# One encoder layer on one core: the up-projection by seven quarter products, activations parked in DRAM, the down-projection as three sweeps

## The chip, the core and the metric

The kernel runs on one core of a Trainium2 chip. The metric is the device time of one execution in microseconds (us). TensorE (PE) multiplies, VectorE (DVE), ScalarE (ACT) and GpSimd (POOL) work on its results, and SyncE (SP) issues the transfers between DRAM and the chip. All data are float32.

## The reference, cut to what matters

The program is one layer of a streaming encoder for 1024 prompt tokens and 32 sample tokens: an input projection, two kinds of attention, an output projection with a first norm, a gated feed-forward with a causal convolution of width 3, a second norm, and a gated embedding. The change concerns the feed-forward:

```python
def _conv_ffn(h, conv_state, lp):
    u = h @ lp['w_up']                       # (tokens, 1024) @ (1024, 5632)
    up = jnp.concatenate([conv_state, u], 1)
    z = lp['conv_b'] + sum(up[:, j:j + s] * lp['conv_w'][j] for j in range(CONV_W))
    g, v = z[..., :D_FF], z[..., D_FF:]      # D_FF = 2816
    out = (jax.nn.gelu(g, approximate=False) * v) @ lp['w_down']   # (tokens, 2816) @ (2816, 1024)
...
h = _ln(ALPHA * x + a, lp['ln1_g'], lp['ln1_b'])
f, new_conv = _conv_ffn(h, conv_state, lp)
h = _ln(ALPHA * h + f, lp['ln2_g'], lp['ln2_b'])
gate = jax.nn.sigmoid(h @ lp['w_ple_gate'] + lp['b_ple_gate'])
y = h + gate * (p_emb @ lp['w_ple_proj'])
```

## The kernel before

**Products.** TensorE reads its operands as float32r, a shorter form of float32. Each operand is therefore kept as two parts: `split` copies the high part on ScalarE (L85) and subtracts it from the source on VectorE or GpSimd (L82). `three` (L144 to L146) then sums three matmuls for each pair of 128x128 tiles: high by high, high by low, low by high.

**Layout.** Features lie on the partitions, tokens along the columns: 1024 prompt tokens, 2 spare columns and 32 sample tokens make T = 1058. On-chip memory is cut into pools: `G` (8 large tiles), `WP` (6 tiles of half that size, `pair`), `SL` (4, `slab`) and `ST` (2, `stg`). Every weight tile that `wload` brings in passes through one of the two `ST` buffers: a load (L112), a copy on ScalarE, a subtraction on VectorE or GpSimd; then the buffer is free again.

**Order.** A scheduler orders each engine's instructions when the program is built: what is written first goes first, as soon as its inputs and a buffer are there. Each engine then runs its list in that order and waits only for data and buffers. `held` and `load` keep an instruction, in that order, behind the one that `gate[0]` names.

**Up.** After the output projection, `h_rows` makes the normed rows of a block of 128 tokens (the two products with g and b of the norm run on GpSimd, L1038 and L1039, but for the last block), `h_cols` turns them on TensorE (L1068) and writes both parts into `hT`. The up-projection then takes 44 feature tiles, gate and value of a feature in turn. For each, `up_block` runs three blocks of 352 or 354 token columns, 24 matmuls each, with the weights as the stationary operand, and ScalarE copies the sum out (L1097). `conv` makes three VectorE operations of it (L1110, L1112). `glu` applies GELU and multiplies; `keep` splits the result into `acts`.

**Down.** Features are taken in groups of four. While the next group's up-projection runs, `down` multiplies the group before with its rows of w_down: for each block of tokens and each half of 512 columns, three matmuls per feature, then an addition into the row sums in `acc` on VectorE (L1153). So up- and down-projection alternate, and the weights of the one come in under the products of the other. Before the last stage, the weights of the gate are loaded (`wg`) while the last groups are multiplied.

**Last stage.** `y_norm` adds the last two features and norms the rows, `y_cols` turns and splits them, `y_rows` multiplies with the gate's weights and writes the output; six blocks of rows are normed ahead.

## Time and profile before

| what | us |
|---|---|
| median of 3 runs | 1627.09 (1626.44 to 1627.8) |
| span of the profiled execution | 1620.0 |
| TensorE busy in it | 1564.6 (97%) |
| VectorE, ScalarE, GpSimd busy | 843.5, 597.1, 352.3 |

The span runs from the first instruction to the last of one profiled execution; what that execution took outside its span is not recorded, so only the timed runs show it. "Busy" counts time in which an engine had at least one instruction under way. A matmul is pipelined: its duration in a row is longer than the distance to the next matmul, and it is that distance that adds up to time.

### The profile page before, as it was taken

To read this page: it belongs to the slowest core of one execution; us is meant where nothing else is said; L and a number is where in the kernel's file an instruction comes from. 1 tells how busy PE (TensorE), PEld (TensorE's weight loads), DVE (VectorE), ACT (ScalarE), POOL (GpSimd) and SP (SyncE) were. 2 spreads that over 40 slices of the span, in tenths; PEclk is the share of its full clock that TensorE was granted. 3 is DMA by queue.
4 is the path that set the end of the run, shared out by engine and by line. 5 is a ranking of instruction groups with operands and counts; after the bars stand their busy time and mean duration, and the time that the engine had idled before them with its cause. 6 is when DMAs were issued, how large, how long until landed. Compare 5 with 4: busy or idle time off the path is not lost.

```text
span 1620.0 us, 23579 instructions
## 1 busy us (share of the span) xinstructions
PE 1564.6 (97%) x9486; PEld 1429.8 (88%) x9486; DVE 843.5 (52%) x1505; ACT 597.1 (37%) x1339; POOL 352.3 (22%) x432
## 2 busy tenths in 40 slices
PE   8999998889989999999999999999999999999998
PEld 7999987778878899999979988997998899876887
DVE  4112328887777665755444443544444354688322
ACT  4222438887787750233303321330332133232111
POOL 0002225633464202810000000000000000038511
PEclk9999999999999999999999999999999999999999
DMA  7121252220111162011102111110211111140001
GB/s 238 44 59 41 79 166 46 63 54 8 45 43 37 31 226 55 27 53 53 40 13 79 40 39 53 53 40 13 79 40 40 52 53 40 40 156 17 35 34 40
DMA packets 95506, 95.58 MB, mean 59 GB/s; under 512 B 10733, under 2 KB 80997, under 8 KB 95141
## 3 DMA queue, kind: packets, MB, share of 16 engines
q1 hardware_dynamic: 95397, 94.07, 19.0%
q8 instruction: 75, 1.23, 0.3%
q14 instruction: 34, 0.28, 0.1%
HBM read 77.74 MB, written 9.96 MB: 54 GB/s over the span
## 4 chain that ended last, share of the span: by engine, by line
PE 81%; DVE 9%; ACT 4%; DMA 3%; POOL 1%; issue 1%; SPq 0%; ACTq 0%; DVEq 0%; POOLq 0%
PE pm L144 23%; PE pm L145 23%; PE pm L146 23%; PE pm L810 2%; DVE w L521 1%; DVE w L559 1%; DVE g L82 1%; PE pm L801 1%; PE pm L152 1%; PE pm L153 1%; ACT w L85 1%; PE pd L144 1%; DMA t<-in_w_o 1%; DVE w L82 1%; ACT g L85 1%
## 5 line engine op out<-in xcount | busy, mean ns | idle before, releaser
L144 PE MATMUL pm<-g,w 128*128 128x352 f32 (+2 forms) x1300 | 425.8, 328 | 2.4 <-DVE w L82 1.1
L145 PE MATMUL pm<-g,w 128*128 128x352 f32 (+2 forms) x1300 | 424.9, 327 | 0.1
L146 PE MATMUL pm<-g,w 128*128 128x352 f32 (+2 forms) x1300 | 422.3, 325 | 0.4 <-DVE w L82 0.4
L144 PE MATMUL pm<-w,g 128*128 128x256 f32 (+2 forms) x896 | 296.4, 331 | 5.7 <-DVE sm L176 3.0
L146 PE MATMUL pm<-w,g 128*128 128x256 f32 (+2 forms) x896 | 293.8, 328 | 0.4 <-DVE g L82 0.2
L145 PE MATMUL pm<-w,g 128*128 128x256 f32 (+2 forms) x896 | 293.1, 327 | 0.0
L144 PEld LDWEIGHTS pm<-g,w 128*128 128x128 f32 x1300 | 245.3, 189 | 5.5 <-DVE w L82 1.6
L145 PEld LDWEIGHTS pm<-g,w 128*128 128x128 f32 x1300 | 246.0, 189 | 1.6 <-DVE g L82 0.9
L146 PEld LDWEIGHTS pm<-g,w 128*128 128x128 f32 x1300 | 245.9, 189 | 1.6 <-DVE w L82 0.9
L144 PEld LDWEIGHTS pm<-w,g 128*128 128x128 f32 x896 | 169.9, 190 | 24.7 <-DVE sm L176 3.6
L85 ACT CAST w<-t 128x1024 fp32r<-128x1024 f32 (+2 forms) x97 | 100.9, 1041 | 228.0 <-PE pm L146 187.2
L146 PEld LDWEIGHTS pm<-w,g 128*128 128x128 f32 x896 | 168.6, 188 | 16.7 <-DVE g L82 1.0
L145 PEld LDWEIGHTS pm<-w,g 128*128 128x128 f32 x896 | 169.0, 189 | 15.5 <-issue 0.5
L1107 POOL COPY ucol<-s 128x2 f32<-128x2 f32 x44 | 31.5, 716 | 635.0 <-ACT s L1097 635.0
L1097 ACT COPY s<-pm 128x352 f32<-128x352 f32 x132 | 59.9, 454 | 279.9 <-PE pm L146 279.8
L82 DVE TENSOR_TENSOR w<-t,w 128x1024 fp32r<-128x1024 f32 (+2 forms) x91 | 111.2, 1222 | 97.1 <-ACT w L85 97.1
L1110 DVE TENSOR_SCALAR s<-s,cp 128x1058 f32<-128x1058 f32 x44 | 36.6, 832 | 232.5 <-ACT s L1097 232.5
L1112 DVE SCALAR_TENSOR_TENSOR s<-s,cp,s 128x1058 f32<-128x1058 f32 x88 | 115.9, 1318 | 1.6
L1153 DVE TENSOR_TENSOR g<-pm,g 128x512 f32<-128x512 f32 x96 | 64.6, 682 | 88.3 <-PE pm L146 88.2
L82 DVE TENSOR_TENSOR w<-pm,w 128x512 fp32r<-128x512 f32 (+3 forms) x124 | 61.3, 515 | 19.0 <-ACT w L85 18.4
L85 ACT CAST w<-pm 128x512 fp32r<-128x512 f32 (+3 forms) x124 | 53.2, 450 | 48.2 <-PE pm L801 18.6
L119 POOL TENSOR_SCALAR s<-s,sm 128x1024 f32<-128x1024 f32 (+8 forms) x56 | 45.3, 811 | 106.1 <-DVE sm L783 65.1
(291 smaller groups left out, 2386.6 us busy)
## 6 DMA issues: line engine op xcount, KB each, us to landing
t<-in_w_up SPq DMA_DIRECT2D x44, 512.0 KB, 3.7
t<-in_w_down SPq DMA_DIRECT2D x22, 512.0 KB, 3.2
g<-in_x_p SPq DMA_DIRECT2D x15, 512.0 KB, 9.7
t<-in_w_in SPq DMA_DIRECT2D x14, 512.0 KB, 3.8
t<-in_w_o SPq DMA_DIRECT2D x8, 512.0 KB
t<-in_w_gate SPq DMA_DIRECT2D x8, 512.0 KB, 3.3
out_y_p<-t SPq DMA_DIRECT2D x16, 256.0 KB, 2.0
g<-g SPq DMA_DIRECT2D x6, 512.0 KB, 4.3
```

The lines of the kernel that those rows point to most:

```text
L82: return eng.tensor_tensor(out, x, y, ALU.subtract)
L85: c = ACT.copy(hi, src)
L119: return eng.tensor_scalar(out, x, s, 0.0, ALU.mult, ALU.add)
L144: PE.matmul(ps, sh, mh, start=(i == 0), stop=False)
L145: PE.matmul(ps, sh, ml, start=False, stop=False)
L146: PE.matmul(ps, sl, mh, start=False, stop=(i == last))
L810: PE.matmul(po[:, c : c + 256], vt[:, k, h % 4], pts[k // 4][:, hl, k % 4], start=(k == 0 and hl == 0), stop=(k == kt - 1 and hl == 1))
L1097: ACT.copy(U[:, 2 + c0 : 2 + c0 + n], ps[:, :n])
L1107: POOL.tensor_copy(ucol[:, 0:2, m], U[:, 1024:1026])
L1110: DVE.tensor_scalar(z, U[:, 0:T], cp[:, 0, m : m + 1], cp[:, 3, m : m + 1], ALU.mult, ALU.add)
L1112: DVE.scalar_tensor_tensor(z, U[:, j : j + T], cp[:, j, m : m + 1], z, ALU.mult, ALU.add)
L1153: DVE.tensor_tensor(d, ps[:n], d, ALU.add)
```

## The change

`G` and `WP` become one pool `HP` of 22 tiles of the smaller size (`pair`; what was a `G` tile is now two of them).

The up-projection treats two neighbouring feature tiles at once. The weights of the pair (1024 rows, 256 columns) and the tokens are each cut into 2 x 2 quarters: rows by halves of 512, columns by the two feature tiles, tokens into two halves of 128 within each pair of blocks. `up_stage` makes four sums of weight quarters on GpSimd, `combos` four sums of token quarters; of the eleven terms on either side, seven products of quarters suffice (Strassen's scheme in Winograd's form), added up partly in PSUM and partly on VectorE. Each of the 22 pairs runs 7 products for 2 sets of tokens, 12 matmuls of 264 columns each. The split token terms, `hC`, take 14 of the 22 tiles.

The gated activations go to DRAM (`zd`); the normed rows go to DRAM too (`hrow`) and their tiles are given up. After the whole up-projection the rows come back, and the down-projection runs as sweeps over the blocks of tokens with 8, 10 and 4 features; a sweep loads its rows of w_down first, then for each block the activations from DRAM, which it splits (`z_in`). The third sweep is part of the last stage's `y_norm`; its weights, the gate's weights, three tables and `w_proj` are loaded ahead of it. Loads of the sweeps are held behind the last addition of the up-projection. Elsewhere, tiles are addressed as two halves and otherwise used as before.

```diff
-    G = ctx.enter_context(tc.tile_pool(name="G", bufs=8))
-    WP = ctx.enter_context(tc.tile_pool(name="WP", bufs=6))
+    HP = ctx.enter_context(tc.tile_pool(name="HP", bufs=22))
...
+        return HP.tile(list(shape), dt, tag="h", name=nm("h"))
+    def gpair(dt=F32):
+        return [pair((128, 2, T), dt) for _ in range(2)]
...
+    hrow = [DR.tile([128, 1024], F32, name=nm("hrow")) for _ in range(8)]
...
+        if t < 8:
+            SP.dma_start(hrow[t], arow(t))
...
+    def combos(b11, b12, b21, b22, t4, dst):
+        t1, t2, t3, t4 = t4
+        ACT.copy(t4, b12)
+        b12 = t4
+        sub(DVE, t1, b12, b11)
+        sub(DVE, t2, b22, t1)
+        sub(DVE, t3, b22, b12)
+        sub(DVE, t4, b21, t2)
+        for i, src in enumerate((b11, b21, t2, t3, t1, t4, b22)):
+            split(*dst(i), src, POOL if i in (2, 4) else None)
...
+    def h_pair(b, q):
+        t = 4 * (1 - b) + 2 * q
+        p0, p1 = h_turn(t), h_turn(t + 1)
+        hc_tiles(b)
+        tt = pair((128, 4, 4, 128), F32)
+        cs = slice(128 * q, 128 * q + 128)
+        combos(p0[:, 0:4], p1[:, 0:4], p0[:, 4:8], p1[:, 4:8], [tt[:, j] for j in range(4)],
+               lambda i: (hC[b, i][:, :, 0, cs], hC[b, i][:, :, 1, cs]))
...
-    def up_w(m):
-        return wload([(0, 1024, w_up[:, :, m * 128 : (m + 1) * 128])], 1024)
-    def up_block(w, U, b):
-        wv_ = w[:, :, :1024].rearrange("p h (k c) -> p h k c", k=8)
-        c0, n = NB[b]
+    def up_stage(m):
+        R, S = pair((128, 8, 256), F32), pair((128, 4, 4, 128), F32)
+        load(R, w_up[:, :, m * 128 : m * 128 + 256])
+        a11, a21 = R[:, 0:4, 0:128], R[:, 0:4, 128:256]
+        a12, a22 = R[:, 4:8, 0:128], R[:, 4:8, 128:256]
+        s1, s2, s3, s4 = (S[:, j] for j in range(4))
+        POOL.tensor_tensor(s1, a21, a22, ALU.add)
+        sub(POOL, s2, s1, a11)
+        sub(POOL, s3, a11, a21)
+        sub(POOL, s4, a12, s2)
+        return (a11, a12, s2, s3, s1, a22, s4)
+    def up_part(src, i, room=None):
+        w = room or (stg if i in (1, 4) else slab)((128, 2, 4, 128), F32R)
+        split(w[:, 0], w[:, 1], src[i])
+        return w
+    class UpPair:
+        def __init__(self, m):
+            self.m = m
+            self.U = pair((128, 2, T + 2), F32)
+            held(POOL.memset(self.U[:, :, 0:2], 0.0))
+            self.ps = {}
+        def at(self, j, b, h):
+            u = self.U[:, j]
+            v = u[:, 2:1026].rearrange("p (x h c) -> p x h c", h=2, c=128)
+            s = 2 + S0 + 16 * b + 8 * h
+            return v[:, 2 * (1 - b) : 2 * (1 - b) + 2, h], u[:, s : s + 8]
+        def read(self, ps, j, b, h, add):
+            d, ds = self.at(j, b, h)
+            v, vs = ps[:, :256].rearrange("p (x c) -> p x c", c=128), ps[:, 256:BW]
+            for x, y in ((d, v), (ds, vs)):
+                if add:
+                    UnitF[0] = DVE.tensor_tensor(x, y, x, ALU.add)
+                else:
+                    ACT.copy(x, y)
+        def product(self, w, i, b):
+            if i == 0 and (0, b) not in self.ps:
+                x = pd()
+                self.ps[0, 0], self.ps[0, 1] = self.ps.get((0, 0), x), x[:, 512:]
+            if i in (1, 3):
+                self.ps[i, b] = pm()
+            ps = self.ps[0 if i % 2 == 0 else 3 if i == 5 else i, b]
+            first = i in (0, 1, 3)
+            for k in range(4):
+                c = hC[b, i]
+                PE.matmul(ps[:, :BW], w[:, 0, k], c[:, k, 0], start=first and k == 0, stop=False, skip_group_check=True)
+                PE.matmul(ps[:, :BW], w[:, 0, k], c[:, k, 1], start=False, stop=False, skip_group_check=True)
+                PE.matmul(ps[:, :BW], w[:, 1, k], c[:, k, 0], start=False, stop=k == 3, skip_group_check=True)
+            j, h, add = ((0, 0, False), (0, 0, True), (1, 0, False), (1, 1, False), (1, 1, True), (1, 0, True), (0, 1, False))[i]
+            self.read(ps, j, b, h, add)
+        def conv(self):
+            U, m = self.U, self.m
+            z = pair((128, 2, T), F32)
+            for j in range(2):
+                ACT.copy(U[:, j, S0 : S0 + 2], cp[:, 4:6, m + j])
+                POOL.tensor_copy(ucol[:, 0:2, m + j], U[:, j, 1024:1026])
+                POOL.tensor_copy(ucol[:, 2:4, m + j], U[:, j, T : T + 2])
+                ACT.activation(z[:, j], U[:, j, 0:T], AF.Identity, bias=cp[:, 3, m + j : m + j + 1], scale=cp[:, 0, m + j : m + j + 1])
+                for i in (1, 2):
+                    DVE.scalar_tensor_tensor(z[:, j], U[:, j, i : i + T], cp[:, i, m + j : m + j + 1], z[:, j], ALU.mult, ALU.add)
+            return z
+    UnitF = [None]
+    def up(m, src):
+        u = UpPair(m)
+        for i in range(NP):
+            w = up_part(src, i)
+            for b in range(2):
+                u.product(w, i, b)
+        return u.conv()
+    GROUPS = [list(range(0, 8)), list(range(8, 18)), list(range(18, 22))]
+    zd = [DR.tile([128, len(fs), T], F32, name=nm("zd")) for fs in GROUPS]
+    ms = [m + e for m in range(0, NF, 2) for e in (0, NF)]
+    for t in order[:4]:
+        h_rows(t)
+    hs = slab()
+    V["hs"], V["hs2"] = hs[:, :256].rearrange("p (k c) -> p k c", k=8), hs[:, 256:512]
+    ACT.copy(V["hs"], h_turn(8)[:, :, :DEC])
+    h_rows(4)
+    h_pair(0, 1)
+    h_sample(0)
+    h_rows(3)
+    h_pair(0, 0)
+    src = up_stage(ms[0])
+    h_rows(2)
+    h_rows(1)
+    first = [pair((128, 2, 2, 4, 128)) for _ in range(3)]
+    wfirst = [up_part(src, i, first[i // 2][:, i % 2] if i < 6 else None) for i in range(NP)]
+    h_rows(0)
+    u = UpPair(ms[0])
+    u.ps[0, 0] = pm()
+    for i in range(4):
+        u.product(wfirst[i], i, 0)
+    h_pair(1, 1)
+    h_sample(1)
+    for i in range(4, NP):
+        u.product(wfirst[i], i, 0)
+    h_pair(1, 0)
+    for i in range(NP):
+        u.product(wfirst[i], i, 1)
+    src = up_stage(ms[1])
+    zg = u.conv()
+    gate[0] = None
+    for n, m in enumerate(ms):
+        if n:
+            z = up(m, src)
+        if n + 1 < len(ms):
+            nxt = up_stage(ms[n + 1]) if n else src
+        src = nxt
+        if n % 2 == 0:
+            zg = z if n else zg
+            ACT.activation(zg, zg, AF.Gelu)
+        else:
+            POOL.tensor_tensor(zg, zg, z, ALU.mult)
+            fi = m - NF
+            g = next(g for g, fs in enumerate(GROUPS) if fi in fs)
+            i = fi - GROUPS[g][0]
+            SP.dma_start(zd[g][:, i : i + 2, :], zg)
+    gate[0] = UnitF[0]
+    acc = [pair((128, 2, 1024), F32) for _ in range(4)]
+    def wdown(fs, eng=None):
+        return [wload([(0, 1024, w_dn[:, fi])], 1024, eng) for fi in fs]
+    def z_in(g, t):
+        c0, n = TOK[t]
+        K = len(GROUPS[g])
+        kn = K if K <= 8 else K // 2
+        ds = []
+        for k0 in range(0, K, kn):
+            d = pair((128, kn, 2, n))
+            st = stg((128, kn, 128))
+            load(st[:, :, :n], zd[g][:, k0 : k0 + kn, c0 : c0 + n])
+            split(d[:, :, 0], d[:, :, 1], st[:, :, :n])
+            ds += [d[:, k] for k in range(kn)]
+        return ds
...
-    def keep(fi, zg):
-        if fi % 2 == 0:
-            acts[fi // 2] = gtile([128, 2, 2, T])
-        d = acts[fi // 2][:, fi % 2]
-        split(d[:, 0], d[:, 1], zg)
...
-    half, fs = groups[-2][:2], groups[-1]
-    down(half, ws[:2])
-    for fi, zf in zip(fs, z):
-        keep(fi, zf)
-    ws, wlast = wdown(fs, None), ws[2:]
-    down(groups[-2][2:], wlast)
...
+    for t in order[1:]:
+        load(arow(t), hrow[t])
+    for g in range(2):
+        ws = wdown(GROUPS[g])
         for t in order:
+            z = z_in(g, t)
             for c in (0, 512):
+                down_rows(g, t, ws, z, c)
...
+    ws = wdown(GROUPS[2])
+    w_gate = a["w_gate"].rearrange("(k p) c -> p k c", p=128)
+    wg = [wload([(0, 1024, w_gate[:, k])], 1024, POOL if k % 2 else None) for k in range(8)]
+    tabs = [pair((128, 2, T), F32) for _ in range(2)]
...
+        z = z_in(2, t)
         for c in (0, 512):
-            down_rows(t, fs, ws, c, asam)
-        norm(arow(t)[: TOK[t][1]], TOK[t][1], tabs[:, 0], tabs[:, 1])
+            down_rows(2, t, ws, z, c)
```

## Rows read from the trace of the kernel before

**Rows 1.** the page: span, busy time of each engine, granted TensorE clock by slice

```profile
span 1620.0 us, 23579 instructions
...
PE 1564.6 (97%) x9486; PEld 1429.8 (88%) x9486; DVE 843.5 (52%) x1505; ACT 597.1 (37%) x1339; POOL 352.3 (22%) x432
...
PEclk9999999999999999999999999999999999999999
```

**Rows 2.** the page: the chain that ended last, shares by engine

```profile
PE 81%; DVE 9%; ACT 4%; DMA 3%; POOL 1%; issue 1%; SPq 0%; ACTq 0%; DVEq 0%; POOLq 0%
```

**Rows 3.** busy time by stretch (us): busy time and instructions, clock, DMA, GB/s

```profile
200.00:575.00 375.00, 340.89 (x2270) 298.67 (x2269) 267.93 (x713) 270.71 (x711) 162.32 (x185) 0.99 0.21 57
700.00:1400.00 700.00, 700.00 (x3952) 659.92 (x3951) 317.44 (x311) 177.10 (x292) 40.57 (x128) 1.00 0.14 44
```

**Rows 4.** TensorE in order of time: start, us, line, shape; 256, 288, 352, 512 columns

```profile
596.56 0.29 PE L144 MATMUL pm<-w,g 128*128 128x256 f32 x1
...
602.02 0.28 PE L145 MATMUL pm<-w,g 128*128 128x256 f32 x1
...
113.00 0.29 PE L144 MATMUL pm<-w,g 128*128 128x288 f32 x1
...
119.91 0.29 PE L145 MATMUL pm<-w,g 128*128 128x288 f32 x1
...
903.89 0.32 PE L144 MATMUL pm<-g,w 128*128 128x352 f32 x1
...
908.89 0.32 PE L145 MATMUL pm<-g,w 128*128 128x352 f32 x1
...
954.28 0.39 PE L144 MATMUL pm<-w,g 128*128 128x512 f32 x1
...
971.93 0.39 PE L145 MATMUL pm<-w,g 128*128 128x512 f32 x1
```

**Rows 5.** instructions by line and shape, 700 to 1400: busy, mean ns

```profile
L1112 DVE SCALAR_TENSOR_TENSOR s<-s,cp,s 128x1058 f32<-128x1058 f32 x86 | 113.3, 1318 | 1.6
...
L82 DVE TENSOR_TENSOR w<-t,w 128x1024 fp32r<-128x1024 f32 x58 | 70.8, 1221 | 20.2 <-ACT w L85 20.2
```

**Rows 6.** instructions by line and shape, 575 to 700

```profile
L82 DVE TENSOR_TENSOR g<-pd,g 128x256 fp32r<-128x256 f32 x31 | 12.8, 415 | 4.9 <-ACT g L85 4.8
```

**Rows 7.** GpSimd in order of time, norms of the rows

```profile
645.67 2.39 POOL L1038 TENSOR_TENSOR g<-g,s 128x1024 f32<-128x1024 f32 x1 [0.64 <-DVE g L1037]
...
684.53 3.33 POOL L1038 TENSOR_TENSOR g<-g,s 128x1024 f32<-128x1024 f32 x1 [1.06 <-DVE g L1037]
```

**Rows 8.** the chain of waits around 1413 us: start, us, what

```profile
1413.36 3.23 DMA t<-in_w_gate
1416.61 1.06 ACT g L85
1417.70 1.24 DVE g L82
1418.95 3.25 DMA t<-in_w_gate
```

**Rows 9.** VectorE in order of time, the same operation twice

```profile
642.71 2.88 DVE L1037 TENSOR_SCALAR g<-g,sm 128x1024 f32<-128x1024 f32 x1 [0.61 <-POOL sm L177]
...
656.99 0.81 DVE L1037 TENSOR_SCALAR g<-g,sm 128x1024 f32<-128x1024 f32 x1 [0.26 <-POOL sm L177]
```

**Rows 10.** busy time by stretch where the first up products start

```profile
690.00:700.00 10.00, 7.81 (x45) 6.78 (x44) 8.10 (x13) 4.28 (x13) 3.14 (x5) 0.91 0.35 105
700.00:710.00 10.00, 10.00 (x59) 10.00 (x58) 2.96 (x5) 2.32 (x5) 0.89 (x2) 0.92 0.01 2
```

**Rows 11.** busy time by stretch, where many loads are queued

```profile
575.00:600.00 25.00, 23.85 (x193) 22.86 (x193) 19.37 (x46) 16.27 (x44) 0.10 (x1) 1.00 0.84 314
```

**Rows 12.** busy time by stretch, end of the feed-forward and start of the last stage

```profile
1435.00:1440.00 5.00, 3.85 (x17) 2.82 (x16) 5.00 (x7) 1.02 (x3) 0.95 (x1) 1.00 0.38 113
1455.00:1480.00 25.00, 21.38 (x100) 16.21 (x99) 23.95 (x55) 3.65 (x14) 15.99 (x12) 0.93 0.15 48
```

More of the change, by code (lines that the diff above doesn't have):

```diff
@@ L159, in compact @@
             kk = min(2, nk - 2 * i)
-            ACT.copy(d[:, 2 * i : 2 * i + kk], f(g[:, :kk, :, S0:T]))
+            for p in range(2):
+                ACT.copy(d[:, 2 * i : 2 * i + kk, p], f(g[p][:, :kk, S0:T]))
         return d.rearrange("p k h c -> p k (h c)")
@@ L281, in layer @@
     dv_s, cc_s = rows_s[:, :512], rows_s[:, 512:]
-    cc = gtile([128, 8, 512], F32)
+    cc = [pair((128, 4, 512), F32) for _ in range(2)]
     ksl = slab()
@@ L496, in layer @@
     steps += prep_b(0)
-    dv = gtile([128, 8, 512], F32)
+    dv = [pair((128, 4, 512), F32) for _ in range(2)]
     for blk in range(2):
@@ L651, in keys_init @@
     def keys_init():
-        L["QK"] = QK = [gtile([128, 2, 2, T]) for _ in range(2)]
+        L["QK"] = QK = [[pair() for _ in range(2)] for _ in range(2)]
         L["krs"] = krs = cpool.tile([128, DEC], F32R, name="krs")
@@ L741, in block @@
             else:
-                split(QK[1][0:64, which, 0, cs], QK[1][0:64, which, 1, cs], ps[64:128, :n])
+                split(QK[1][which][0:64, 0, cs], QK[1][which][0:64, 1, cs], ps[64:128, :n])
             if c0 + n == T:
@@ L918, in sa_end @@
         for e in range(2):
-            ACT.copy(L["mixA"][64 * e : 64 * e + 64, :, S0:T], v[64 * e : 64 * e + 64, :, e])
+            for g in range(2):
+                ACT.copy(L["mixA"][g][64 * e : 64 * e + 64, :, S0:T], v[64 * e : 64 * e + 64, 2 * g : 2 * g + 2, e])
     w_o = a["w_o"].rearrange("(k p) c -> p k c", p=128)
@@ new lines, in layer @@
+    h_pair(1, 0)
+    for i in range(NP):
+        u.product(wfirst[i], i, 1)
[17 more added lines that the diff above has]
+            SP.dma_start(zd[g][:, i : i + 2, :], zg)
@@ new lines, in layer @@
+    gate[0] = UnitF[0]
+    acc = [pair((128, 2, 1024), F32) for _ in range(4)]
+    def wdown(fs, eng=None):
[12 more added lines that the diff above has]
+        return ds
@@ L1278, in layer @@
         y_norm(t)
-        p_in(t)
     y_cols(order[0])
```

295 lines of the change are left out of this document (113 added, 182 removed).

## The prediction, made before the change was run

> **What bounds the kernel now.** I read the page first: TensorE is busy for 97% of the span, its clock is granted in full in nearly every slice, and no other engine passes 52% [rows 1]. The chain of waits agrees: 81% of it is TensorE [rows 2]. By stretches, attention leaves TensorE 34 us idle, while from 700 to 1400 us, up- and down-projection, it has no gap at all [rows 3]. There only fewer or cheaper matmuls can save time, and every wait put into this stretch costs its full length. So I price the matmuls by the distance between their starts: 0.1187 us at 256 columns (46 steps from 596.56 to 602.02), 0.1329 at 288 (52 steps), 0.1613 at 352 (31 steps), 0.2322 at 512 (76 steps) [rows 4]. That is nearly a straight line: columns set the price, plus some 5 ns each.
>
> **Up-projection.** Removed: 44 tiles x 72 = 3168 matmuls, of which 2112 have 352 columns and 1056 have 354 (0.1613 x 354/352 = 0.1622): 340.7 + 171.3 = 512.0 us. Added: 22 pairs x 7 products x 2 token sets x 12 = 3696 matmuls of 264 columns. No row has 264, so it lies between 0.1187 and 0.1329; on the line between them it is 0.1222, which I take, 264 being nearest to 256. That makes 451.7 us, a gain of 60.3 (ends: 73.3 and 20.8). The down-projection keeps its matmuls.
>
> The Trainium skill's page "TensorE: Matmul & The Clock Gate", section "Back-to-back issue gap", gives sustained spacings of 81 ns at 128 columns and 131 at 512. By a line through these, an estimate, 264 columns cost 99 ns and 352 cost 110, and the up-projection would grow from 349 to 365 us; the trace has 232 ns at 512 and contradicts it.
>
> **Is the up-projection still bound by TensorE?** A pair takes 168 x 0.1222 = 20.5 us. VectorE: a subtraction costs 0.415 us at 256 elements and 1.221 at 1024 [rows 5, 6], so about 0.68 at 512. Seven such (4.8), six additions out of PSUM of 256 elements (0.42 each) and six tiny ones, some 3.5, and four convolution steps at 1.318 [rows 5] (5.3) make 13.6 us. GpSimd: 1024 elements take 2.39 [rows 7], so four weight sums of 512 take 4.8; half a product of 2116 elements, 2.5; with small copies, some 8.2 us. ScalarE: seven copies of 512, eight of 256, eight tiny ones, two passes and one GELU of 1058, some 12.5 us by its 1.06 for 1024 elements [rows 8]. Each engine alone fits. But VectorE and GpSimd get in each other's way: the same VectorE operation took 2.88 us while a GpSimd sum ran, and 0.81 without [rows 9]. If all GpSimd work held VectorE up, its 13.6 would become 21.8 of 20.5. I take +4 us over all pairs, since six product buffers run ahead; ends 0 and 24.
>
> The Trainium skill's page "SBUF — State Buffer", section "SBUF: two separate sides", says that the two share a pair of ports and that one blocks the other for a whole instruction. By that rule alone the sum would take the upper end, +24; the trace agrees that waits of this kind exist.
>
> **Start of the up-projection.** GpSimd's norms come every 6.5 us per block of rows (six steps from 645.67 to 684.53), two operations of 2.39 in each, and slow to 3.33 per operation at the end [rows 7]. In front of the last norm on GpSimd now also come four weight sums (4.8) and four splits of token terms (4.8): some 7 us later after the slack. Block 0's root is queued behind it there, then come its norm on VectorE, two turns, and `combos`, nine dependent VectorE steps at 0.68. TensorE can cover 84 x 0.1222 = 10.3 us with products of the first token set. I reckon about 13.5 us idle plus 2 at the lower clock, where before there were 2.2 idle and 1.7 lost because the clock, halved for a moment, averaged 0.91 and 0.92 over 20 us [rows 10]. Cost +12; ends +4 (products cover the rest) and +26 (VectorE held up throughout).
>
> **Seam before the first sweep.** Here lies the main cost. The up-projection keeps 14 of 22 tiles for token terms, and its weights, sums and results need the other 8. So nothing of the sweeps can be loaded before, and TensorE has no other work. The loads: eight blocks of rows (4.2 MB) and two weight tiles (1.0 MB) at 314 GB/s [rows 11] take 17 us. They are ordered behind the last addition, 2.9 us before the end of the products, but the queue may start them sooner where a tile is free; I place the second weight tile at 7 us, when VectorE has also done the last convolution (5.3). Then all eight weight tiles and the first activations pass through the two staging buffers. One turn of a buffer is 3.23 load + 1.06 copy + 1.24 subtraction, 5.59 from load to load [rows 8]. First pair split at 9.5; three more turns, 26.3; the first activations, 3.6: 30 us. Ends 23 (everything in place at the end of the products) and 37 (nothing started before the gate).
>
> **First to second sweep.** A block takes 48 x 0.2322 = 11.1 us of TensorE against 2.8 per staged tile, so the next weights come in as tiles fall free; the last of ten and the first activations need a turn after that: 3 us, ends 0 and 6.
>
> **Seam before the last stage.** While the second sweep's last block runs (60 x 0.2322 = 13.9 us), the tiles are full: 4 of rows, 10 of weights, 2 of activations, 2 of tables (loaded early, needing no staging buffer), 4 of third-sweep weights. Two gate tiles wait in the staging buffers. Weights are freed only in the last half, from 6.3 us before the end. Then ten tiles (eight gate, two `w_proj`) go through the buffers, all written ahead of the first activations of the third sweep. Six of the ten are subtracted on GpSimd (2.39 instead of 1.24), so a turn is 5.6 or 6.8, 6.2 on average. First pair at -2.8, four turns, +22; the activations squeeze in one tile early: TensorE starts 23 us late. Ends 26, and 5 if the activations are queued ahead of the gate weights.
>
> **Smaller terms.** After each of the two long seams the clock must rise again: 1.7 us each by [rows 10], 3.4 together (ends 0 and 7). Embedding rows turned later, just before their use: +1 (0 to 5). What vanishes: 1.2 us of gaps before 1440 and, at the start of the last stage, 3.6 idle and 1.8 at a clock of 0.93 [rows 12]: -6.6 (ends -6.6 and -1.2). The activations' splits only change place. Transfers of 12 MB out and 12 in ride under products: a block needs 0.52 MB per 11.1 us, 47 GB/s. The regrouped tiles and some ten extra tiny ScalarE copies in attention I cost at nothing, hidden by the 104 us that ScalarE is idle there [rows 3]; bare they cost 2 us. More freely shared tiles could as well save a few of TensorE's 34 idle us: -5 to +5.
>
> **Sum.** -60.3 + 4 + 12 + 30 + 3 + 23 + 3.4 + 1 - 6.6 = +9.5 us. On the profiled span: 1620.0 + 9.5 = 1629.5. The timed median lies 7.1 us above that span; this rest stays, so 1636.6.
>
> **Rivals.** What a run can tell from no change is about 0.2%, 3.3 us.
>
> *The last seam is short, and the kernel is faster.* If the third sweep's first activations get a staging buffer ahead of the gate weights, that seam falls from 23 to 5, and the time is 1636.6 - 18 = 1618.6; with the first seam at its lower end too, 1612. It decides once the seam is under 10 us. For it: the gate weights are needed only six blocks later. Against it: weights came in as written before, and TensorE never had to wait for that. Chance 0.32, range 1604 to 1623.
>
> *No change.* The seams come out 6 to 13 us shorter in sum: 1624 to 1630. Chance 0.12.
>
> *The up-projection is bound by VectorE and GpSimd.* The 24 of the upper end instead of 4: 1657. For it: [rows 9]. Against it: between 700 and 1400 VectorE is busy for 317 of 700 us and its buffers run ahead. Chance 0.11.
>
> *Each matmul keeps a price of its own.* At the 288-column price the gain is 20.8: 1676. The even line of [rows 4] speaks against it. Chance 0.02. The skill's spacing rule above would have this direction.
>
> *My forecast*, gain real but eaten by seams: chance 0.43, its own range 1631 to 1660.
>
> **How the numbers follow.** Slower: 0.43 + 0.11 + 0.02 = 0.56; same 0.12; faster 0.32. The forecast is that of the likeliest case, 1636.6. The range runs from 1606, which leaves out less than 1 in 10 below (the far half of the fast case), to 1664, past the case bound by VectorE, leaving out 1 in 10 above.
>
> **What would show it.** Right: starts of 264-column matmuls 0.122 us apart; a pair every 20.5 to 21 us; TensorE idle for some 30 us between the last product and the first sweep, some 3 before the second, some 23 before the last stage, with a lower granted clock after each; staged loads of the gate weights ending that last gap. Wrong: gaps under half of these; a spacing over 0.13; VectorE without a pause and TensorE gaps inside the pairs; or attention changed by over 5 us.

## The result, and the profile after

The changed kernel takes 1934.3 us (median of four runs, 1931.5 to 1935.5) beside 1626.8 of the kernel before on the same chip: 1.1894 times as long, 95% interval 1.1877 to 1.191. The forecast was 1636.6, range 1606 to 1664. Slower was right; 298 us of the time were not foreseen. One of the six executions of a later run (the residual rows spread) took 1899.5 us in a slower state of the chip, at a clock of 0.744, and is left out of its median.

The page after, with span, busy time of each engine, and TensorE's busy share and granted clock in 40 slices; it answers to [rows 1]:

```profile
span 1929.8 us, 25535 instructions
...
PE 1620.0 (84%) x10014; PEld 1447.3 (75%) x10014; DVE 975.1 (51%) x1756; ACT 704.5 (37%) x1708; POOL 555.4 (29%) x521
...
PE   8999988898997986768778687877773999959999
...
PEclk9999999899998997888878888887977999989999
```

TensorE's row on the page of the kernel before:

```profile
PE   8999998889989999999999999999999999999998
```

The span is 310 us longer, and TensorE's share falls from 97% to 84%. From slice 13 to slice 30 (579 to 1447 us) a row that was nearly all 9 before reads mostly 6 to 8, and the clock falls with it. No engine took TensorE's place: VectorE has 51%. Time that no engine fills is waiting.

Four stretches of it, columns as in [rows 3]: the output projection, the up-projection, and the two seams.

```profile
600.00:610.00 10.00, 0.23 (x1) 0.23 (x2) 2.06 (x3) 2.68 (x5) 0.00 (x0) 0.66 0.77 287
900.00:1150.00 250.00, 189.10 (x1243) 177.94 (x1244) 130.40 (x172) 81.41 (x206) 79.87 (x69) 0.83 0.16 51
1470.00:1500.00 30.00, 1.91 (x5) 1.12 (x6) 15.65 (x10) 7.00 (x8) 5.55 (x1) 0.50 0.69 235
1720.00:1740.00 20.00, 1.18 (x3) 0.74 (x4) 1.52 (x2) 4.50 (x6) 9.32 (x4) 0.57 0.55 189
```

The second line is the one to read: TensorE idle for 61 of 250 us, clock 0.83, and VectorE busy for 130, ScalarE for 81, GpSimd for 80. In [rows 3] TensorE had 700.00 of 700. The 1243 matmuls took 250 / 1243 = 0.201 us each, a pair of feature tiles (168 of them) 33.8 us instead of the 20.5 forecast. Of the 13.3 too much, 8.2 are idle (60.9 / 250 x 33.8). In the other 5.1 TensorE is busy, but with matmuls that take 189.1 / 1243 = 0.152 us each in the mean; most of it is the lower clock, at which they start 0.22 us apart (from 933.69 to 935.45 us, for one) and not 0.122 (from 923.63 to 924.73). Over twenty-one such pairs the 13.3 add up to 280 us.

Who TensorE waits for, over the whole run (us in total, times, longest):

```profile
PE pd L1195 <- DVE s L82: 54.5, 20, 3.5
PE pm L152 <- DVE h L82: 52.8, 2, 31.4
PE pd L1193 <- ACT s L85: 46.8, 20, 2.3
PE pm L1195 <- DVE t L82: 25.2, 10, 2.5
```

The two long waits of L152 are the seams that the prediction worked out, 31.4 and 21.3 us (forecast 30 and 23). New are above all the three others, 126.5 us: the parts of a pair's weights, first the high part that ScalarE casts (L85), then the low part that VectorE subtracts (L82). One border of two pairs, TensorE first (start, us, what, and in brackets the idle time before it and what ended it):

```profile
923.28 0.39 PE L1193 MATMUL pd<-h,s 128*128 128x264 f32 x1 [0.59 <-DVE h L1178]
...
925.54 0.39 PE L1193 MATMUL pd<-h,s 128*128 128x264 f32 x1 [0.53 <-ACT h L1180]
...
929.60 0.39 PE L1193 MATMUL pd<-h,s 128*128 128x264 f32 x1 [2.34 <-ACT s L85]
...
933.30 0.59 PE L1195 MATMUL pd<-h,s 128*128 128x264 f32 x1 [2.43 <-DVE s L82]
...
938.38 0.59 PE L1195 MATMUL pm<-h,t 128*128 128x264 f32 x1 [2.51 <-DVE t L82]
```

ScalarE at the same border:

```profile
927.30 0.44 ACT L1180 COPY h<-pd 128x256 f32<-128x256 f32 x2 [1.81 <-PE pd L1195]
927.77 1.27 ACT L1208 ACTIVATE h<-h,cp 128x1058 f32<-128x1058 f32 x1
928.95 0.60 ACT L85 CAST s<-h 128x512 fp32r<-128x512 f32 x1
929.46 0.61 ACT L85 CAST t<-h 128x512 fp32r<-128x512 f32 x1
...
935.91 0.44 ACT L1180 COPY h<-pd 128x256 f32<-128x256 f32 x2 [5.13 <-PE pd L1195]
```

And VectorE:

```profile
924.61 2.68 DVE L1210 SCALAR_TENSOR_TENSOR h<-h,cp,h 128x1058 f32<-128x1058 f32 x2 [1.39 <-ACT h L1208]
929.08 3.57 DVE L1210 SCALAR_TENSOR_TENSOR h<-h,cp,h 128x1058 f32<-128x1058 f32 x2 [1.78 <-ACT h L1208]
932.57 0.68 DVE L82 TENSOR_TENSOR s<-h,s 128x512 fp32r<-128x512 f32 x1
933.17 6.84 DVE L82 TENSOR_TENSOR t<-h,t 128x512 fp32r<-128x512 f32 x2
```

The last product of the old pair is read at 927.30, and in that queue the convolution's first step (L1208) comes next. Only then, at 928.95, is the first part of the new pair cast. On VectorE four convolution steps (L1210) end at 932.65, and behind them stand the first low part (932.57) and two more, which take 6.84 us together while GpSimd runs its 5.05 us multiply from 932.73 on. So TensorE gets its weights one by one, 2.3 to 2.5 us late each. No sum and no part of the new pair is made while the old one multiplies: the border is a chain through three engines, none of which is busy.

### The profile page after: what moved, and what is told of

Same layout as the page of the kernel before. It is cut to its first block, busy times and chain, and to the rows that moved or that the text cites. A ratio compares the mean times of both kernels' runs of the same rounds, so it can differ in the third digit from the quotient of the medians.

```text
span 1929.8 us, 25535 instructions
## 1 busy us (share of the span) xinstructions
PE 1620.0 (84%) x10014; PEld 1447.3 (75%) x10014; DVE 975.1 (51%) x1756; ACT 704.5 (37%) x1708; POOL 555.4 (29%) x521
## 5 line engine op out<-in xcount | busy, mean ns | idle before, releaser
L144 PE MATMUL pm<-h,h 128*128 128x256 f32 (+4 forms) x1140 | 378.7, 332 | 16.4 <-ACT h L85 11.9
L146 PE MATMUL pm<-h,h 128*128 128x256 f32 (+4 forms) x1140 | 375.4, 330 | 1.7 <-DVE h L82 1.7
L145 PE MATMUL pm<-h,h 128*128 128x256 f32 (+4 forms) x1140 | 374.8, 329 | 0.0
L144 PEld LDWEIGHTS pm<-h,h 128*128 128x128 f32 x1140 | 217.7, 191 | 36.0 <-ACT h L85 12.9
L146 PEld LDWEIGHTS pm<-h,h 128*128 128x128 f32 x1140 | 216.0, 190 | 18.7 <-DVE h L82 2.1
L145 PEld LDWEIGHTS pm<-h,h 128*128 128x128 f32 x1140 | 216.6, 190 | 16.9 <-issue 0.5
L1193 PE MATMUL pd<-h,s 128*128 128x264 f32 x508 | 163.2, 321 | 71.1 <-ACT s L85 46.8
L1195 PE MATMUL pd<-h,s 128*128 128x264 f32 x508 | 160.4, 316 | 54.5 <-DVE s L82 54.5
L85 ACT CAST h<-t 128x1024 fp32r<-128x1024 f32 (+6 forms) x97 | 88.3, 919 | 263.2 <-PE pm L146 148.6
L82 DVE TENSOR_TENSOR h<-t,h 128x1024 fp32r<-128x1024 f32 (+6 forms) x87 | 97.3, 1126 | 163.6 <-ACT h L85 163.1
L1193 PEld LDWEIGHTS pd<-h,s 128*128 128x128 f32 x508 | 106.9, 211 | 84.8 <-ACT s L85 51.0
L1210 DVE SCALAR_TENSOR_TENSOR h<-h,cp,h 128x1058 f32<-128x1058 f32 x88 | 134.3, 1527 | 70.2 <-ACT h L1208 68.7
L1194 PE MATMUL pd<-h,s 128*128 128x264 f32 x508 | 155.2, 306 | 0.0
L1195 PEld LDWEIGHTS pd<-h,s 128*128 128x128 f32 x508 | 107.8, 212 | 59.8 <-DVE s L82 59.8
L82 POOL TENSOR_TENSOR h<-h,h 128x512 f32<-128x512 f32 (+2 forms) x84 | 130.8, 1561 | 30.1 <-ACT h L484 21.4
L82 DVE TENSOR_TENSOR h<-pm,h 128x256 fp32r<-128x256 f32 (+7 forms) x221 | 101.6, 485 | 56.4 <-ACT h L85 54.5
L85 ACT CAST h<-pm 128x256 fp32r<-128x256 f32 (+7 forms) x221 | 88.2, 425 | 53.8 <-PE pm L804 21.7
L1194 PEld LDWEIGHTS pd<-h,s 128*128 128x128 f32 x508 | 107.2, 211 | 0.0
L1208 ACT ACTIVATE h<-h,cp 128x1058 f32<-128x1058 f32 x44 | 55.9, 1271 | 125.9 <-DVE h L1178 82.8
```

Of the source, the lines that this page charges most:

```text
L82: return eng.tensor_tensor(out, x, y, ALU.subtract)
L85: c = ACT.copy(hi, src)
L144: PE.matmul(ps, sh, mh, start=(i == 0), stop=False)
L145: PE.matmul(ps, sh, ml, start=False, stop=False)
L146: PE.matmul(ps, sl, mh, start=False, stop=(i == last))
L1193: PE.matmul(ps[:, :BW], w[:, 0, k], c[:, k, 0], start=first and k == 0, stop=False, skip_group_check=True)
```

## The experiments

### What holds up the border of two pairs

Four runs each took one suspect out. The first leaves out the sums on GpSimd:

```diff
...
-        POOL.tensor_tensor(s1, a21, a22, ALU.add)
-        sub(POOL, s2, s1, a11)
-        sub(POOL, s3, a11, a21)
-        sub(POOL, s4, a12, s2)
-        return (a11, a12, s2, s3, s1, a22, s4)
+        return (a11, a12, a21, a21, a11, a22, a12)
```

> The weight sums on GpSimd (four of 512 elements per pair, 8.2 us) and their tile are left out; the parts of all seven products are split straight from the loaded quarters, so the products are those of other weights. Theory A (the sums of the next pair stand in GpSimd's queue behind the copies of this pair's last columns, so the parts come late): pairs fall from 33.65 us to 20.5 to 23 us, TensorE over 95% busy at full clock between the first and the last product, the kernel about 1934 - 21 x 11 = 1700 us or less (1670 to 1720). Theory B (VectorE and GpSimd hold each other up on the subtractions and the gated multiply): only the sums' share of that goes, 4 to 6 us per pair, the kernel 1810 to 1850. Theory C (a matmul of 264 columns costs more than its columns): pairs stay near 33 us, the kernel 1930.

The next takes from GpSimd the copies that wait for a pair's last reads, ahead of the sums in its queue:

```diff
-                POOL.tensor_copy(ucol[:, 0:2, m + j], U[:, j, 1024:1026])
-                POOL.tensor_copy(ucol[:, 2:4, m + j], U[:, j, T : T + 2])
+                ACT.copy(ucol[:, 0:2, m + j], U[:, j, 1024:1026])
+                ACT.copy(ucol[:, 2:4, m + j], U[:, j, T : T + 2])
```

> The four copies of a pair's last columns go to ScalarE's queue; GpSimd keeps sums, clearing and gated multiply in the same order, VectorE's order is untouched (its subtractions for the next pair still stand behind this pair's convolution). Theory A with GpSimd's queue alone as the cause: the sums come some 15 to 25 us earlier, most of the idle time goes, the kernel 1700 to 1780. Theory A with VectorE's queue as the cause (the subtractions behind the four convolution steps): sums early, TensorE still waits 8 us per pair, the kernel 1880 to 1934. Theory B: unchanged within 1%, 1915 to 1950.

The third moves the multiply (`POOL.tensor_tensor(zg, zg, z, ALU.mult)` to `DVE`):

> The gated multiply (2116 elements, 5.05 us on GpSimd every second pair) goes to VectorE. Theory A: the copies still hold up the sums; of the 67.3 us per two pairs only the delay of the last two sums goes, 2 to 5 us, the kernel 1880 to 1915. Theory B: VectorE's subtraction that took 5.15 us beside the multiply falls to about 1 and the multiply takes about 2.5 to 3 there, 5 to 12 us per two pairs, the kernel 1810 to 1880.

The fourth leaves out two of three taps (`for i in (1, 2)` to `for i in ()` in `conv`):

> The second and third tap of the convolution (four VectorE instructions of about 1.4 us per pair, 5.5 to 6.3 us) are left out, so the gated activations are those of a one-tap convolution; the order of the rest is unchanged. Theory D: the chain at the border is shorter by these 5.5 to 6.3 us, less what the parts' casts on ScalarE still take (2 us), and the clock falls less: 4 to 7 us per pair, the kernel 1790 to 1850. Theory A in its first form (the sums stand behind the copies in GpSimd's queue): no change, 1925 to 1940.

And two runs change only the order. One writes the next pair's load and sums ahead of this pair's products:

```diff
         if n:
+            nxt = up_stage(ms[n + 1]) if n + 1 < len(ms) else None
             z = up(m, src)
-        if n + 1 < len(ms):
-            nxt = up_stage(ms[n + 1]) if n else src
-        src = nxt
+            src = nxt
```

> The load and the sums of the next pair are written ahead of this pair's products instead of behind its convolution, so that GpSimd has them before the copies that wait for this pair's last reads; the work is the same. Theory A: pairs of 21 to 24 us, the kernel 1670 to 1740. Theory B: the same instructions still meet, pairs of 30 us or more, the kernel 1870 to 1934. Theory C: no change, 1930.

The other does that, and puts a pair's convolution behind the second product of the next pair (`finish` holds the convolution, GELU or multiply, and the store):

```diff
...
+            u = UpPair(m)
+            for i in range(NP):
+                w = up_part(src, i)
+                for b in range(2):
+                    u.product(w, i, b)
+                if i == 1:
+                    finish(n - 1, last)
...
```

> The same work in another order: the load and the sums of the next pair stand ahead of this pair's products, and this pair's convolution, activation, multiply and store are written behind the second product of the next pair. Theory D (the border of two pairs is a chain: last product, its read, the convolution on ScalarE and VectorE, and behind these in the same two queues the parts of the next pair): with the parts ahead of the convolution TensorE has its next weights at the border, pairs of 20.5 to 23 us, clock over 0.97 in the up-projection, the kernel 1650 to 1710. Theory B (VectorE and GpSimd hold each other up, whatever the order): pairs of 27 us or more, 1790 or more. Theory E (the accumulators of a pair in PSUM allow no running ahead): pairs of 24 to 26 us, 1720 to 1780.

Measured (one run each in the five middle rows, medians in the first and last; ratios to the kernel before on the same chip); the last three columns are the stretch from 900 to 1150 us:

| kernel | time, us | of the kernel before | matmuls | TensorE busy | clock |
|---|---|---|---|---|---|
| as changed | 1934.3 | 1.189 | 1243 | 189 | 0.83 |
| multiply on VectorE | 1942.9 | 1.198 | 1192 | 177 | 0.84 |
| copies on ScalarE | 1905.5 | 1.175 | 1324 | 199 | 0.85 |
| no sums | 1900.6 | 1.172 | 1298 | 192 | 0.88 |
| no taps | 1890.7 | 1.163 | 1334 | 192 | 0.90 |
| sums ahead | 1827.7 | 1.127 | 1483 | 204 | 0.93 |
| convolution deferred | 1675.2 | 1.030 (1.028 to 1.033) | 2052 | 250 | 1.00 |

My first theory, that GpSimd's queue delays the sums, fell: without any sums the kernel is only 1.7 points faster, and with the copies out of the way 1.4. Moving the multiply made nothing faster either, but that alone does not refute theory B: at a border of that run the two later low parts take 1.28 us together and not 6.84, so GpSimd had held VectorE up; the multiply (3.30 us) now stands ahead of the first low part in VectorE's own queue, and TensorE waits 6.82 us for that. The taps are 2.6 points, also less than I expected. Without them ScalarE's half of the chain stays (a wait of 2.34 us), and GpSimd's multiply starts earlier, so that the first low part beside it takes 4.75 us in place of 0.68 and TensorE waits 3.51. None of these pieces is the cause alone; what one leaves free, the next in a queue takes up. What all of these left as it was is the order, in which the parts of the next pair stand behind the reads and the convolution of this one. Writing the sums ahead moves the parts up as well, but leaves a rest, which its trace shows. TensorE, then ScalarE:

```profile
1005.13 0.59 PE L1193 MATMUL pd<-h,s 128*128 128x264 f32 x1 [3.06 <-ACT h L1180]
```

```profile
1002.43 0.63 ACT L85 CAST s<-h 128x512 fp32r<-128x512 f32 x1
1002.95 1.28 ACT L1208 ACTIVATE h<-h,cp 128x1058 f32<-128x1058 f32 x1
1004.12 0.61 ACT L85 CAST t<-h 128x512 fp32r<-128x512 f32 x1
1004.63 0.45 ACT L1180 COPY h<-pd 128x256 f32<-128x256 f32 x2
```

Now the parts come first and a read stands behind the convolution: the accumulator that TensorE needs is read at 1004.63, behind L1208 and two casts, and TensorE stands for 3.06 us until then. With the convolution deferred this goes too; two stretches of that run, the start and the middle of the up-projection:

```profile
700.00:800.00 100.00, 79.53 (x566) 75.26 (x565) 83.15 (x113) 42.85 (x111) 57.99 (x47) 0.86 0.22 74
900.00:1150.00 250.00, 250.00 (x2052) 249.86 (x2051) 199.26 (x283) 129.80 (x336) 134.03 (x115) 1.00 0.22 78
```

The whole middle is free of gaps at full clock, with every instruction of the changed kernel still there. VectorE is busy for 199 of 250 us and GpSimd for 134, more densely than in the slow kernel. On each of the four engines both profiles count the same number of instructions. So theories B and E, that the engines or the accumulators set the pace, are out: 259 us were order alone. Writing the sums ahead brings some 100 of them; deferring the convolution without that was not run. ScalarE, where the casts of new parts (t) now come between the reads and ahead of L1208:

```profile
1004.95 0.42 ACT L1180 COPY h<-pd 128x256 f32<-128x256 f32 x2
1005.26 0.64 ACT L85 CAST t<-h 128x512 fp32r<-128x512 f32 x1
1006.54 0.62 ACT L85 CAST t<-h 128x512 fp32r<-128x512 f32 x1 [0.64 <-PE pd L1195]
1007.15 1.27 ACT L1208 ACTIVATE h<-h,cp 128x1058 f32<-128x1058 f32 x1
1008.33 0.42 ACT L1180 COPY h<-pd 128x256 f32<-128x256 f32 x2
```

The price of a product is measured here too: 250 / 2052 = 0.1218 us (forecast 0.1222).

### The seams

The activations of the last sweep's first two blocks ahead of the gate weights, alone in the changed kernel and with the deferred convolution:

```diff
     ws = wdown(GROUPS[2])
+    z2 = {t: z_in(2, t) for t in order[:2]}
...
-        z = z_in(2, t)
+        z = z2.get(t) or z_in(2, t)
```

> The activations of the last sweep's first two token blocks are staged and split ahead of the eight gate weights in place of behind them; nothing else is changed. If the seam before the last stage (21.4 us, TensorE waiting for VectorE's part of the activations) is the staging order, 15 to 20 us go, the kernel 1912 to 1920 (ratio to the changed kernel 0.990). Rival: the last sweep then waits for the gate weights or the residual rows instead, 0 to 5 us go, 1928 to 1934.

> The edits of the two runs before together. If they sit in different stages and don't meet, their gains add: the kernel 15 to 20 us below the reordered one alone, 1630 to 1695 under theory D.

Both gained nothing: 1936.1 (1.1913, 1.1888 to 1.1937) and 1676.3 (1.0315, 1.0292 to 1.0337). The 21.3 us wait did go, but TensorE's first two blocks of the last sweep were followed by these (TensorE, then GpSimd):

```profile
1748.94 1.06 PE L1369 MATMUL pd<-ident,acc_s 32*128 32x32 f32 x8 [16.36 <-POOL acc_s L1042]
1753.20 1.97 PE L1369 MATMUL pd<-ident,h 128*128 128x128 f32 x8 [3.20 <-POOL h L1042]
```

```profile
1733.20 2.34 POOL L82 TENSOR_TENSOR h<-t,h 128x1024 fp32r<-128x1024 f32 x1 [5.19 <-ACT h L85]
...
1740.00 2.34 POOL L82 TENSOR_TENSOR h<-t,h 128x1024 fp32r<-128x1024 f32 x1 [3.08 <-ACT h L85]
1742.29 2.33 POOL L1041 TENSOR_TENSOR acc_s<-acc_s,h 32x1024 f32<-32x1024 f32 x1
...
1746.89 1.99 POOL L1042 TENSOR_TENSOR acc_s<-acc_s,h 32x1024 f32<-32x1024 f32 x1
```

The turn of the first block's rows now waits 16.36 us for GpSimd's norm, which stands in GpSimd's queue between the subtractions of gate weights, and these come as the staging buffers bring them. The wait had moved one step along the same supply. The next run widens the supply: the weights pass through the four slabs instead of the two staging tiles, the residual rows are loaded behind the first sweep's weights, and two blocks of activations come ahead of the weights in both sweeps.

```diff
+    def wslab(src, eng=None):
+        st = slab()
+        load(st[:, :1024], src)
+        return parts(st, 1024, eng)
     def wdown(fs, eng=None):
-        return [wload([(0, 1024, w_dn[:, fi])], 1024, eng) for fi in fs]
+        return [wslab(w_dn[:, fi], eng) for fi in fs]
...
-    for t in order[1:]:
-        load(arow(t), hrow[t])
+    z0 = {t: z_in(0, t) for t in order[:2]}
```

> The reordered kernel with the weights of the sweeps, of the gate and of the last projection staged through the four slabs (free by then) in place of the two staging tiles, the activations of the first two token blocks written ahead of the weights in the first and the last sweep, and the residual rows loaded behind the first sweep's weights. If the two seams are staging turns and the order of loads, the first falls from 31.5 to 12 to 18 us, the last from 21 to 5 to 12, the kernel 1640 to 1655. Rival: the seams are bound by the memory's rate (382 GB/s in the first), 5 to 10 us go, 1665 to 1670.

1641.6 us (1.0105, 1.007 to 1.0141), 34 less. TensorE's first wait at each seam, first and last:

```profile
1213.66 1.12 PE L152 MATMUL pm<-h,h 128*64 128x512 f32 x2 [4.02 <-ACT h L85]
```

```profile
1451.67 0.79 PE L144 MATMUL pm<-h,h 128*128 128x512 f32 x1 [6.72 <-ACT h L85]
...
1456.62 0.50 PE L146 MATMUL pm<-h,h 128*128 128x512 f32 x1 [1.31 <-DVE h L82]
```

From 31.4 and 21.3 us to 4.0 and 6.7, with 1.0 and 1.3 more soon after. The memory's rate was not the bound. Which of the three edits did how much was not taken apart.

### Attention and the output projection

The first residual came 11.3 us later in the changed kernel (593.87 against 582.59), the last one 36.0 (721.82 against 685.85). The regrouped tiles alone, under the feed-forward of the kernel before:

```diff
...
-    hT = [gtile([128, 2, 2, T]) for _ in range(4)]
+    hT = [gpair(F32R) for _ in range(4)]
...
-            acts[fi // 2] = gtile([128, 2, 2, T])
+            acts[fi // 2] = gpair(F32R)
...
```

> One part of the change alone: the tiles of the kernel before are taken from the one pool of 22 pair tiles (each tile of four as two pairs, keys of all heads in one pair), the feed-forward stays that of the kernel before (eight products, no parking, down-projection between). Theory R (the 15 us that the end of attention came later in the changed kernel, and the 10 us that the output projection waits for its weights behind the row loads, come from the regrouping): first residual near 599 in place of 585, the kernel 1640 to 1655. Rival: the regrouping costs nothing, as the prediction had it, and the delay comes with the new feed-forward's demands on the same tiles: 1622 to 1632.

1692.2 us (1.0425, 1.0393 to 1.0456). The first residual is at 596.78, so the delay of attention does come with the regrouping. The wait of the output projection, the other half of theory R, does not: from first to last residual it is 101.9 us here, no longer than in the kernel before (103.3). Most of the remaining loss belongs to this hybrid alone: its up-projection waits 45.7 us, in seven waits of up to 7.5, for ScalarE's casts of weights, which the changed kernel doesn't do. One tile is not only addressed in halves but used otherwise: for the later three differential heads the two maps share one tile of keys, where the kernel before had a tile for each. That as the cause:

```diff
-            if m == 0:
+            if m == 0 or h:
                 V["k"] = pair()
```

> The kernel with the reordered convolution and the seams' loads reordered, and for the later three differential heads a pair tile of keys for each map in place of one for both, which is nearer to the tiles before the change. If the shared key tile is what delays attention by 13 us (its second map's keys wait until the first map's are read), 6 to 13 us go: 1628 to 1636. Rival: the delay comes from the other tiles of the one pool (values, mixed heads, parts of the weights), 0 to 3 us go, 1638 to 1643.

1642.2 (1.0105, 1.0082 to 1.0127): no change. Which tile delays attention stays open.

The output projection stands almost still from 600 to 610 us (0.23 busy of 10 above, 10.00 in the kernel before). Its next weights are loaded behind eight loads of residual rows.

> The reordered kernel (convolution behind the second product of the next pair) with the second block of the output projection's weights loaded ahead of the nine residual rows. If TensorE's 10.3 us wait at 600 to 611 and the half clock behind it are the queue of loads, 10 to 14 us go: 1661 to 1666. Rival: the rows are then late for the residuals of the first block instead, 0 to 4 us go.

1677.2 (1.0326, 1.03 to 1.0351). The trace shows the eight rows still ahead of the weights: the lines of the text had moved, the order of the loads had not. So this run says nothing on the theory. The next one did change the order (`x_rows` loads the rows it is given):

```diff
+    x_rows(order[:3])
     wb.append(wo_block(256, 256))
...
+            if i == 0 and 0 < m < 7:
+                x_rows(order[m + 2 : m + 3])
```

> The same kernel with two residual rows loaded ahead of the second half of the output projection's weights and the other six one by one between the blocks of the first pass, so that the loads' order changes (in the run before that moved only the text, it came out as it was). If TensorE's 10.3 us at 600 to 611 are the weights behind eight row loads (331 GB/s, 12 us), they go and half clock with them: 10 to 14 us, 1628 to 1632. Rival: another tile or cast sets that wait, 0 to 4 us go.

> All edits together: the parts are in different stages, so gains add; 1612 to 1630 if both theories hold, 1628 to 1640 if one does. If it comes below 1623 it beats both kernels, with 20 us of slow start of the up-projection still in it.

1633.4 (1.0053, 1.0033 to 1.0073) and 1634.7 (1.0059, 1.004 to 1.0078); the key tiles add nothing here either. From 600 to 610 TensorE is busy for 7.06 us instead of 2.42, and from first to last residual it is 115.7 us instead of 127.9 (before: 103.3). So the loads' order was 12 us there, of which 8 reach the end.

### The start of the up-projection

In the window of 700 to 800 us shown above, the reordered kernel did 566 matmuls and turns; at 0.1218 us these are 69 us of work, so some 31 were lost, where the kernel before had no gap. Without the four subtractions of `combos`:

> The reordered kernel without the four VectorE subtractions that form the sums of activation quarters (16 of 512 columns and their sample columns are left out; the products take single quarters instead). If the start of the up-projection (700 to 800 us, VectorE busy 45 of the first 50) is bound by VectorE, 12 to 20 us go: 1655 to 1663. Rival: the transposes, the casts on ScalarE or the parts on GpSimd bound it, 0 to 5 us go.

1659.8 (one run; 1.022 against 1.030), 15 less, as if VectorE were the bound. But why is it slow there? Its subtractions by where the operands lie, 660 to 760 us of the run with the rows spread (h lies in SBUF, the on-chip memory of the tiles, pd in PSUM, where TensorE adds up its products; count, busy, mean ns):

```profile
L82 DVE TENSOR_TENSOR h<-h,h 128x512 fp32r<-128x512 f32 x14 | 23.5, 1698 | 0.3 <-ACT h L85 0.3
...
L82 DVE TENSOR_TENSOR h<-pd,h 128x512 fp32r<-128x512 f32 x12 | 8.0, 672 | 2.3 <-ACT h L85 2.3
```

The same 512 elements take 1698 ns in the mean with both operands in SBUF and 672 with one in PSUM, while GpSimd runs sums, splits and norms. Two of the first kind, and the instruction that GpSimd has under way when the first begins:

```profile
709.46 2.78 DVE L82 TENSOR_TENSOR h<-h,h 128x512 fp32r<-128x512 f32 x1
...
724.36 0.68 DVE L82 TENSOR_TENSOR h<-h,h 128x512 fp32r<-128x512 f32 x1
```

```profile
708.88 2.81 POOL L1042 TENSOR_TENSOR h<-h,s 128x1024 f32<-128x1024 f32 x1
```

The first ends 0.55 us after GpSimd's instruction; the second, with GpSimd idle from 722.75 to 729.47, takes 0.68 us. So I moved work onto the engine that looked full:

```diff
-            split(*dst(i), src, POOL if i in (2, 4) else None)
+            split(*dst(i), src)
```

> The kernel with the residual rows between the blocks, and the two of seven low parts of the activation sums that GpSimd takes moved to VectorE, so that VectorE does more and GpSimd less (8 instructions of 1.4 to 1.5 us). Theory P (at the start of the up-projection VectorE's subtractions with both operands in SBUF take 1.70 us in the mean against 0.68 with one in PSUM, because GpSimd works in SBUF beside them): the 14 of them come down towards 0.7 to 1.2 and the start of the up-projection is 4 to 10 us shorter: 1623 to 1630. Rival: VectorE is simply full there, so 8 more instructions of 0.68 us make it 3 to 6 us longer: 1636 to 1640.

> The same with the scale and shift of the first norm (1024 elements, 2.5 us each on GpSimd) moved to VectorE for the four token blocks normed last. Theory P: VectorE takes 1.21 us for each and is held up less, another 2 to 8 us go: 1616 to 1626. Rival (VectorE full): 6 instructions of 1.2 us more on it, 1637 to 1645.

> The same with the second norm's scale and shift on VectorE for the first three blocks of the last stage, where GpSimd was busy 39 of 50 us and VectorE 39 of 50. Theory P: 1 to 4 us less than the run before. Rival: no change, within 2 us.

1623.2, 1623.7 and 1622.5 us: 0.9991 (0.9979 to 1.0003), 0.9996 (0.9983 to 1.0008) and 0.9986 (0.9973 to 1.0) of the kernel before. The same group in the first of them, and in the second:

```profile
L82 DVE TENSOR_TENSOR h<-h,h 128x512 fp32r<-128x512 f32 x22 | 23.1, 1078 | 0.0
```

```profile
L82 DVE TENSOR_TENSOR h<-h,h 128x512 fp32r<-128x512 f32 x22 | 16.0, 756 | 0.0
```

Eight more instructions take no more time in sum, so theory P holds for their length. The kernel is 10 us shorter too, as it forecast, but the traces place little of that at the start: from the last product of the output projection to the end of the eighth pair it is 205.8 us in the run with the rows spread, 203.0 in the first of the three and 198.2 in the second. With the norms moved as well, each subtraction is down to 756 ns and the start is shorter again, yet the time is no better (theory P had forecast 2 to 8 us), and the third run can't be told from the second. What follows the up-projection took 428.0, 423.9 and 429.6 us in these three profiled executions, with no edit there, so one trace each can't say where the 10 us lie. Nor is it excluded that they come from GpSimd's own queue, which the first edit made shorter by eight subtractions. The three are level with the kernel before; none is shown to beat it.

## Why the prediction was wrong, step by step

In order of size, by its own terms:

**"Is the up-projection still bound by TensorE?"** is the step that failed. It was costed at +4 with ends 0 and 24, and was 259: the difference between the changed kernel and the same work in another order. The busy times were roughly sound (VectorE 13.6 us a pair forecast, 199.3 / 250 x 20.5 = 16.3 measured; GpSimd 8.2 and 11.0; ScalarE 12.5 and 10.6), and "each engine alone fits" was true. Wrong was "six product buffers run ahead": buffers for products don't help when the weights of the next product are not there. I had added up what each queue holds per pair, and not asked what stands ahead of the next pair's first part in it. The rival that named VectorE and GpSimd had the right place and the wrong mechanism, and its 24 us was an upper end only for busy time.

The Trainium skill's page "PSUM — Partial Sum Buffer", section "Engine vs sequencer instructions", says that the queues of ScalarE, VectorE and GpSimd are strictly first in, first out. The traces agree: the loads of the weights cast at 928.95 us were issued by 875.5 us and take 6.6 us to land, yet ScalarE stood idle for 1.81 us before 927.30 and did not cast them ahead of the read and the convolution's first step.

**Start of the up-projection**: the mechanism was right, VectorE held up; the size was not. Forecast +12, ends 4 and 26. In the reordered kernel, whose span is 55.7 us over that of before, it is what remains when the terms below are taken off (55.7 + 61.8 for the products - 52.5 for the seams - 12.8 - 12 + 2.2, the forecast's small terms): about 42. In its trace the 1344 products of the first eight pairs take 206.9 us, counted from the last product of the output projection (715.0 to 921.9 us); at 0.1218 each they would take 163.7, and turns are some 4 of the 43 between. So nearly all of the remainder is lost there.

The Trainium skill's page "SBUF — State Buffer", section "SBUF: two separate sides", which the prediction weighed, limits the blocking to VectorE operations with two SBUF inputs (against a GpSimd operation that reads SBUF), besides its faster modes. This case agrees: 672 ns from PSUM, 1698 from SBUF. I had used the rule for all of VectorE's work alike, where the row of the operand's place would have told which steps of `combos` it strikes.

**Attention at nothing** (-5 to +5) failed in a small way: the first residual is 11.3 us later, 12.8 in the reordered kernel. The **loads of the output projection** were no term at all; 12 us there, by the order of loads.

**The seams** were right: 30, 3 and 23 forecast; 31.4, no gap, and 21.3 measured, and both shrank when their supply was widened. The rival of a short last seam needed more than the order it named: with the activations ahead of the gate weights, GpSimd's norm took the seam's place.

**The products** were right: -60.3 forecast; 3696 x 0.1218 = 450.2, or -61.8, once nothing waits. So the seven products do save their 60 us; in the best order tried, the rest of the change spends as much.

**The 7.1 us from span to timed median** were read as a rest that stays. They are not: an execution of 1931.54 us has a span of 1929.8, and the later runs show 1.7 or 1.8 us as well. The rest of the 7.1 is the difference between executions.

## What to carry to other kernels

When a loop's work per turn changes, write down for each engine's queue what stands between the last read of one turn and the first preparation of the next; if these are links of one chain, busy shares say nothing of the turn's length. Put the preparation of the next turn, and not the finish of this one, first in every queue, and look at the queues of the compiled order, not at the text. Before relieving an engine that looks full, see whether its instructions are long by themselves or by their neighbour.

## What was not expected of the hardware

VectorE's subtraction of 512 float32 elements took 672 ns with an operand in PSUM and 1698 in the mean with both in SBUF while GpSimd worked (756 once GpSimd had less to do). Moving eight such subtractions from GpSimd to the busier VectorE left VectorE's sum for them as it was, 23.1 us for 22 against 23.5 for 14. After waits of 2.34 and 2.43 us, with six matmuls between them, matmuls started 0.22 us apart at a granted clock of 0.50 (933.5 to 936.0 us), the lower of TensorE's two levels (1.2 and 2.4 GHz); from 900 to 1150 us the mean granted clock was 0.83, and matmuls took 5.1 us more per pair besides the 8.2 of waiting. In the seam from 1470 to 1500 us, where TensorE was busy for 1.91 of 30 us, the clock was 0.50 as well.
